# A two-block network on one Trainium2 core: the MoE's overflow branch ahead of its last pair of experts, with a hint for its jump, and the start of RWKV, the router and the layer norms rearranged

## Chip, cores, metric

The kernel runs on one core of a Trainium2 chip. The metric is device time in microseconds, the median of several executions. The profile is one execution taken by the hardware profiler. TensorE (PE) multiplies and transposes, with its weight loads shown as PEld; VectorE (DVE), ScalarE (ACT) and GpSimd (POOL) do the elementwise work; SyncE (SP) issues most transfers.

## The reference, cut to what matters

256 tokens of 1024 features pass through a first block (block-sparse attention, a convolutional feed-forward, RWKV-7 time mixing, a second feed-forward) and a second block of two layers, each a mixer (differential attention in layer 0, sparse latent attention "dsa" in layer 1), attention to a memory, and a hierarchical mixture of 16 experts. The parts that the change touches:

```python
# RWKV-7 (start)
xx = x_prev - x
xr, xw, xk, xv, xa, xg = [x + xx * mu[n] for n in range(6)]
w = -softplus(-(w0 + tanh(xw @ w1) @ w2)) - 0.5
a = sigmoid(a0 + (xa @ a1) @ a2)
g = sigmoid(xg @ g1) @ g2
...
# second block, layer i
h = layer_norm(alpha * h + mix, ...)
h = layer_norm(alpha * h + memory_cross_attention(h, ...), ...)
h = layer_norm(alpha * h + hierarchical_moe(h, ...), ...)
...
# hierarchical_moe: 4 groups of 4 experts
g_logits = t @ w_group + b_group          # best group, its softmax weight
e_logits = (t @ w_expert + b_expert)      # of that group the best two experts
combine = one_hot(expert_id) * top_w
for e in range(16):
    hid = silu(t @ w_gate[e]) * (t @ w_up[e])
    y = y + combine[:, e:e+1] * (hid @ w_down[e])
```

## The kernel before

The kernel is one straight program for the five engines, written with a tile framework: a scheduler orders each engine's instructions by program order and readiness, `tc.issue_after(ins)` puts instructions behind `ins` on its engine, and semaphores come from the data. All products before the MoE that decide the routing are made from a high and a low half in fp32r (`split`: ACT casts, DVE subtracts; three matmuls of `mm3`, L230 to L232) or in plain fp32.

**The MoE (`moe`).** Each expert takes up to 64 tokens. `route` (L1611) multiplies the router's weights with the transposed tokens into 20 rows of logits, copies them out (`lt`, L1613) and transposes them back (L1614). `choose` finds group, experts and each token's place (`pos`) on DVE in tiny instructions, and in the same pass the gate weights `C`, `Co` and the largest count `cnti`. `select` makes 0/1 matrices from `pos` (L1688), `gather` multiplies them with `hh` and `hl`, the two halves of the tokens (L1674 on ACT, L1675 on DVE), into `xg`. The loop over `q` takes two experts side by side: 64 gate and up matmuls (L1736), SiLU and product, four transposes, 32 down matmuls (L1782), the scaled results `Y` (L1789 on ACT, L1790 on DVE), and `scatter` (L1722), which adds them into four PSUM banks `acc`, a round later. `deep_add` (L403) adds the finished `acc` to the residual, and `layer_norm_both` (L407 ff.) normalises the two token halves together.

The experts' 100 MB a layer stream through a ring of 1 MB slots (`MoeQueue`): `fetch` issues on SP the next load as soon as a slot is free, `done` returns a slot after its last matmul. `once(pool, tag, parts, keep)` lends buffers of other pools to the ring; such a slot is used again only while more than `keep` loads remain.

If an expert got more than 64 tokens, `moe_dense` computes the overflow. It stands in `tc.If(over > 64)` at L1775, inside the last round's down matmuls; in these inputs it is jumped over. Every engine loads `over` from `cnti` into a register (L1747) and branches. A branch hint stands after the last round's gate and up matmuls (L1742). After the If, each engine adds to its semaphores what the skipped instructions would have added (EVENT_SEMAPHORE of L1775). Both layers use the label "dense".

**Layer norm.** `layer_norm` runs the token halves t = 0, 1 in turn: DVE adds the residual with a row sum (L372), makes the mean (L374), ACT squares with the mean as bias (L378), DVE scales (L382), two tiny DVE instructions make variance plus epsilon (L383, L384), POOL the power -1/2 (L385), DVE shifts (L391). Then `to_T` transposes (L265), ACT copies out (L277), and `route` follows. `layer_norm_both` has the same steps at L412 to L428.

**RWKV's start (`rwkv`).** After the first feed-forward come six small loads into `prow` (mixing factors and parameter rows), turned by one transpose (L628); the low-rank weights `w1`, `a1`, `g1`; `rms`; the shifted difference `xv` (L656, L657); and `mixed` (L660), one DVE instruction of 128x256 for each slab of 128 features: 8 for `xr`, 8 for `xk`, 24 for the three low-rank inputs of `lora`, whose 24 matmuls are at L671, 8 for the values. The main projections `rkp` (L236) use `xr` and `xk`.

**dsa's start.** Four loads of `b_w_in_2` by `self.load`, a `split` for each of 8 slabs, and three products a slab with the tokens.

## Time and profile before

| what | value |
|---|---|
| median of 3 runs | 1677.26 us (1676.26 to 1682.25) |
| profiled execution: its own time | 1680.34 us |
| its span, first to last instruction | 1678.5 us |
| PE busy | 1584.2 us (94%) |
| DVE busy | 856.2 us (51%) |
| ACT busy | 658.6 us (39%) |
| POOL busy | 63.3 us (4%) |
| mean granted TensorE clock | 0.971 |

Times in rows are microseconds from the start of the span unless marked ns. A line number is the kernel's. `x16` is a count of instructions merged into a row; an fp32 matmul shows as two. What stands in brackets is the engine's idle time before the row and what ended it. PEq, DVEq and so on are the engines' sequencers.

### The profile page before, as it was taken

The numbers are of one execution on the slowest core, as the hardware profiler recorded it, in microseconds if no ns is written. First come the engines' busy times: TensorE is split into PE (matmuls) and PEld (weight loads), VectorE is DVE, ScalarE is ACT, GpSimd is POOL, SyncE is SP. The second block draws the span as 40 slices with busy tenths as digits, with TensorE's granted clock in tenths as the row PEclk, the third lists the DMA queues.
The fourth block names the chain that finished last, engine by engine and source line by source line (L and its number), as shares of the span: only waits on it lengthen the run. The fifth ranks groups of instructions, "written<-read, shape, count | busy, mean of one in ns | idle before, by whom it ended". The sixth has DMA issues, their size and how long they took to land. (4 is left out here: it accounts for less than half of the span.)

```text
span 1678.5 us, 24550 instructions
## 1 busy us (share of the span) xinstructions
PE 1584.2 (94%) x9775; PEld 1160.6 (69%) x9775; DVE 856.2 (51%) x1849; ACT 658.6 (39%) x1236; POOL 63.3 (4%) x80
## 2 busy tenths in 40 slices
PE   7999999989999999999999898999968989899996
PEld 6878999958767659999888685444427768544442
DVE  5777666475665338666558645212226954421122
ACT  5776555323334236554457452111116644211111
POOL 0000000001100000000100200000000020000000
PEclk9999999989899998999999999999989999999998
DMA  9524645333223348653471855999968266599994
GB/s 345 178 76 152 226 158 169 79 92 107 85 75 108 115 138 276 204 173 126 182 270 51 336 193 209 417 416 415 405 250 307 76 239 267 212 416 415 416 416 156
DMA packets 163625, 375.27 MB, mean 224 GB/s; under 512 B 17188, under 2 KB 97836, under 8 KB 148908
## 3 DMA queue, kind: packets, MB, share of 16 engines
q1 hardware_dynamic: 159216, 363.79, 59.3%
q10 hardware_dynamic: 4284, 9.81, 1.7%
q8 instruction: 80, 1.31, 0.3%
q14 instruction: 45, 0.37, 0.1%
HBM read 372.52 MB, written 1.05 MB: 223 GB/s over the span
## 5 line engine op out<-in xcount | busy, mean ns | idle before, releaser
L203 DVE TENSOR_TENSOR wl<-w,wh 128x1024 fp32r<-128x1024 f32 (+1 forms) x221 | 265.0, 1208 | 187.1 <-ACT wh L202 186.6
L202 ACT CAST wh<-w 128x1024 fp32r<-128x1024 f32 (+1 forms) x221 | 227.0, 1038 | 211.1 <-PE mm L231 125.6
L1736 PE MATMUL mm<-mw,xg 128*64 128x512 f32 x1024 | 224.1, 593 | 2.2 <-DMA mw<-in_moe_w_up_dram 2.2
L232 PE MATMUL mm<-xh,wl 128*128 128x256 f32 x688 | 195.7, 284 | 0.0
L231 PE MATMUL mm<-xl,wh 128*128 128x256 f32 x688 | 195.4, 284 | 0.0
L230 PE MATMUL mm<-xh,wh 128*128 128x256 f32 x688 | 194.9, 283 | 0.4 <-ACT wh L202 0.4
L1736 PEld LDWEIGHTS mm<-mw,xg 128*64 128x64 f32 x1024 | 83.5, 137 | 138.7 <-issue 133.4
L230 PEld LDWEIGHTS mm<-xh,wh 128*128 128x128 f32 x688 | 131.1, 191 | 2.4 <-ACT wh L202 0.7
L230 PE MATMUL acc<-wh,xh 128*128 128x512 f32 x324 | 130.3, 408 | 1.7 <-ACT xh L268 1.0
L231 PEld LDWEIGHTS mm<-xl,wh 128*128 128x128 f32 x688 | 130.6, 190 | 1.9
L232 PEld LDWEIGHTS mm<-xh,wl 128*128 128x128 f32 x688 | 130.6, 190 | 0.0
L231 PE MATMUL acc<-wl,xh 128*128 128x512 f32 x324 | 129.3, 400 | 0.0
L232 PE MATMUL acc<-wh,xl 128*128 128x512 f32 x324 | 128.7, 399 | 0.0
L1782 PE MATMUL mm<-mw,hT 128*64 128x512 f32 x512 | 115.6, 595 | 3.1 <-issue 2.2
L1745 DVE TENSOR_TENSOR hid<-hid,mm 128x512 f32<-128x512 f32 x16 | 11.0, 686 | 185.9 <-PE mm L1736 185.9
L1782 PEld LDWEIGHTS mm<-mw,hT 128*64 128x64 f32 x512 | 40.1, 137 | 68.1 <-issue 67.0
L1790 DVE SCALAR_TENSOR_TENSOR Y<-mm,cs,Y 128x512 fp32r<-128x512 f32 x32 | 24.0, 750 | 115.8 <-ACT Y L1789 114.1
L230 PEld LDWEIGHTS acc<-wh,xh 128*128 128x128 f32 x324 | 61.6, 191 | 16.3 <-ACT mv L1290 1.5
L232 PEld LDWEIGHTS acc<-wh,xl 128*128 128x128 f32 x324 | 61.2, 189 | 14.2 <-DVE xl L271 0.3
L231 PEld LDWEIGHTS acc<-wl,xh 128*128 128x128 f32 x324 | 61.5, 190 | 13.1 <-DVE wl L203 0.5
L1789 ACT ACTIVATE Y<-mm,cs 128x512 fp32r<-128x512 f32 x32 | 22.0, 687 | 122.6 <-PE mm L1782 122.6
L232 PE MATMUL acc<-wh,fl 128*128 128x512 f32 x176 | 69.8, 396 | 0.0
(530 smaller groups left out, 2833.5 us busy)
## 6 DMA issues: line engine op xcount, KB each, us to landing
mw<-in_moe_w_down_dram SPq DMA_DIRECT2D x62, 1024.0 KB, 16.0
mw<-in_moe_w_gate_dram SPq DMA_DIRECT2D x58, 1024.0 KB, 8.2
mw<-in_moe_w_up_dram SPq DMA_DIRECT2D x56, 1024.0 KB, 16.8
w<-in_ffn_w_gate_dram SPq DMA_DIRECT2D x22, 1024.0 KB, 8.2
w<-in_ffn_w_up_dram SPq DMA_DIRECT2D x22, 1024.0 KB, 6.4
w<-in_ffn_w_down_dram SPq DMA_DIRECT2D x22, 1024.0 KB, 5.5
w<-in_attn_w_qkv_dram SPq DMA_DIRECT2D x12, 1024.0 KB, 15.5
w<-in_rwkv_w_rkv_dram SPq DMA_DIRECT2D x24, 512.0 KB, 4.0
```

The costliest lines, as they stand in the source:

```text
L202: nc.scalar.copy(r[0], raw)
L203: low = lambda: (lo_eng or nc.vector).tensor_tensor(r[1], raw, r[0], op=ALU.subtract)
L230: mm(out, lhs[0], rhs[0], start=start, stop=False)
L231: mm(out, lhs[0], rhs[1], start=False, stop=False)
L232: mm(out, lhs[1], rhs[0], start=False, stop=stop)
L1736: full = mm(ps[64 * e:64 * e + 64], xg[:, k, q % 2 * 128 + e * 64:q % 2 * 128 + e * 64 + 64], mq.slab(w[2 * (k // 4) + e], k % 4), start=k ...
L1745: tt(hid, hid, gu[1], op=ALU.mult)
L1782: mm(pd[hf][64 * e:64 * e + 64], hT[:, k, 64 * e:64 * e + 64], b, start=k == 0, stop=k == 3)
L1789: act.activation(y[0], pd[hf], AF.Copy, scale=cs)
L1790: vec.scalar_tensor_tensor(y[1], pd[hf], cs, y[0], op0=ALU.mult, op1=ALU.subtract)
```

## The change

The overflow branch now stands at the start of the last round, before its gate and up matmuls, with a label for each layer; `moe_dense` takes its buffers from the pool `gp` instead of `mo` and `xp`, and `gp`'s two slots stay in the weight ring only while more than 14 loads remain. The hint stands in round 6, for PE behind its last transpose and for DVE behind the copy of `hT`, and for no other engine. PE's load of `over` is placed ahead of round 2's matmuls. In the last round the first half's `Y`, its scatter and its `deep_add` stand among the second half's matmuls.

More than the branch is changed. The router's matmul has the tokens as stationary operand and gives the logits token by token, without `lt` and the transpose; the second part of `choose` (gates, `C`, `Co`, `cnti`) is a function `gate` that runs after the first gather; `hh` stands behind the second token half's squares on ACT, `hl` moves from DVE to POOL behind the second half's power. In the last layer norm before the MoE, the copies of the first half's transposes and its `route` wait for the second half's squares and power. All layer norms square with scale 1/32, with one tiny instruction fewer after the squares and one more before them. RWKV's parameter rows and low-rank weights are loaded ahead of the first feed-forward (`rwkv_ahead`) and turned in its fifth round; the low-rank products are split by the identity (x + xx mu) w = x w + xx (mu w): `part` multiplies `x32` with the plain weights, per token half inside `rms`, and `xv` with weights scaled once. For dsa the first two loads of `b_w_in_2` go into buffers of `xp` ahead of the layer norm, and its products run the first token half ahead of the second.

```diff
             if x32 is not None:
-                nc.scalar.copy(x32[sl], pv)
+                if defer is None:
+                    nc.scalar.copy(x32[sl], pv)
+                else:
+                    def full(sl=sl, pv=pv):
+                        with self.tc.issue_after(self.square):
+                            nc.scalar.copy(x32[sl], pv)
+                    defer.append(full)
...
-            nc.vector.tensor_scalar(st[:, 2:3], st[:, 0:1], st[:, 1:2], -1.0 / D, op0=ALU.add, op1=ALU.mult)
+            nc.vector.tensor_scalar(st[:, 3:4], st[:, 0:1], st[:, 1:2], -1.0 / (32 * D), op0=ALU.add, op1=ALU.mult)
+            nc.vector.tensor_scalar(st[:, 2:3], st[:, 3:4], 32.0, None, op0=ALU.mult)
...
-                self.square = nc.scalar.activation(mix[t][hf], x[:, t, sl], AF.Square, bias=st[:, 2:3],
+                self.square = nc.scalar.activation(mix[t][hf], x[:, t, sl], AF.Square, scale=1.0 / 32, bias=st[:, 3:4],
...
-            nc.vector.tensor_scalar(st[:, 3:4], st[:, 6:7], st[:, 7:8], 1.0 / D, op0=ALU.add, op1=ALU.mult)
-            nc.vector.tensor_scalar(st[:, 4:5], st[:, 3:4], 1e-5, None, op0=ALU.add)
+            nc.vector.tensor_scalar(st[:, 4:5], st[:, 6:7], st[:, 7:8], 1e-5, op0=ALU.add, op1=ALU.add)
             self.pow = nc.gpsimd.tensor_tensor(st[:, 5:6], st[:, 4:5], self.mhalf, op=ALU.pow).ins
...
+                if x32 is not None and t == 0:
+                    defer.append(lambda: after(0))
+                else:
+                    after(t)
...
-            vec.tensor_scalar(st[t][:, 3:4], st[t][:, 6:7], st[t][:, 7:8], 1.0 / D, op0=ALU.add, op1=ALU.mult)
-            vec.tensor_scalar(st[t][:, 4:5], st[t][:, 3:4], 1e-5, None, op0=ALU.add)
+            vec.tensor_scalar(st[t][:, 4:5], st[t][:, 6:7], st[t][:, 7:8], 1e-5, op0=ALU.add, op1=ALU.add)
             pool.tensor_tensor(st[t][:, 5:6], st[t][:, 4:5], self.mhalf, op=ALU.pow)
...
+                if j == 4 and extra:
+                    extra()
...
                 if 1 <= j <= nj:
                     down(j - 1, 0)
         self.pending = acc
+
+    def rwkv_ahead(self):
+        nc, i = self.nc, self.i
+        self.wx = ExitStack()
...
+        nc.sync.dma_start(prow[0:48], i["rwkv_mu"][0].rearrange("n (f p) -> (n f) p", p=128))
+        for n, name in enumerate(("rwkv_w0", "rwkv_a0", "rwkv_k_k", "rwkv_k_a")):
+            nc.sync.dma_start(prow[48 + 8 * n:56 + 8 * n], i[name][0].rearrange("(f p) -> f p", p=128))
+        nc.sync.dma_start(prow[80:88], i["rwkv_r_k"][0].rearrange("(f e) d -> f (e d)", e=2))
+        wa1 = x0.tile([128, 8, 128], F32, name="wa1")
...
+            nc.sync.dma_start(t, i[name][0].rearrange("(k p) r -> p k r", p=128))
+        par0 = x0.tile([128, 11, 8], F32, name="par0")
+
+        def turn():
+            p = self.ps()
+            nc.tensor.transpose(p[:, 0:88], prow, self.ident[0:88, 0:88])
...
+        wx = self.wx
+        par0, *low = self.low_rank
         par = one([128, 12, 8], "par")
-        p = self.ps()
-        pe.transpose(p[:, 0:88], prow, self.ident[0:88, 0:88])
-        vec.tensor_copy(par[:, 0:11], p[:, 0:88].rearrange("p (n f) -> p n f", f=8))
+        vec.tensor_copy(par[:, 0:11], par0)
...
-        for u in range(4):
+        for u in range(2):
             wload(u)
-        self.rms(h, i["norm_mix"][1], 1e-6, x32=x32)
-        self.acc_close()
+        mixing = []
+        for wt, parts in zip(low, (((1, 0, 64), (4, 64, 128)), ((5, 0, 128),))):
+            t = self.raws_tile()[:, 0:1024].rearrange("p (k r) -> p k r", k=8)
+            for n, a, b in parts:
+                tt(t[:, :, a:b], wt[:, :, a:b], par[:, MU + n].unsqueeze(2).broadcast_to([128, 8, b - a]), op=ALU.mult)
+            mixing.append(t)
+        for u in range(2, 4):
+            wload(u)
...
+        def part(ws, x, sl, stop):
+            for n, wt in enumerate(ws):
+                for k in range(8):
+                    mm(plr[0][:, n * 256 + sl.start:n * 256 + sl.stop], wt[:, k], x[:, k, sl],
+                       start=x is x32 and n == 0 and k == 0 and sl.start == 0, stop=stop and n == 1 and k == 7)
+
+        def shifted(t):
+            if t == 0:
+                plr.append(self.ps())
+            part(low, x32, slice(t * 128, t * 128 + 128), False)
+            c = max(1, t * 128)
+            for g in range(2):
+                ks = slice(4 * g, 4 * g + 4)
+                tt(xv[:, ks, c:t * 128 + 128], x32[:, ks, c - 1:t * 128 + 127], x32[:, ks, c:t * 128 + 128], op=ALU.subtract)
+                if t == 0:
+                    ts(xv[:, ks, 0:1], x32[:, ks, 0:1], -1.0, None, op0=ALU.mult)
+
+        self.rms(h, i["norm_mix"][1], 1e-6, x32=x32, between=shifted)
+        self.acc_close()
...
         def lora():
-            pw, pa_, pg = self.ps(), self.ps(), self.ps()
-            for k in range(8):
-                for n, wt, p, rows in ((1, w1, pw, slice(0, 64)), (4, a1, pa_, slice(64, 128)), (5, g1, pg, slice(0, 128))):
-                    m = mixed(n, k, x1.tile([128, 256], F32, name="xm", bufs=5))
-                    mm(p[rows, 0:256], wt[:, k], m, start=k == 0, stop=k == 7)
-            act.activation(tw[0:64], pw[0:64, 0:256], AF.Tanh)
-            act.copy(tw[64:128], pa_[64:128, 0:256])
-            act.activation(tg, pg[:, 0:256], AF.Tanh, scale=0.5)
+            part(mixing, xv, slice(0, 256), True)
+            act.activation(tw[0:64], plr[0][0:64, 0:256], AF.Tanh)
+            act.copy(tw[64:128], plr[0][64:128, 0:256])
+            act.activation(tg, plr[0][:, 256:512], AF.Tanh, scale=0.5)
...
-                mm(p[0:20, 0:128], wr[:, k], x32[:, k, t * 128:t * 128 + 128], start=k == 0, stop=k == 7)
-            lt = one([20, 128], "lt")
-            act.copy(lt, p[0:20, 0:128])
-            nc.tensor.transpose(p[:, 128:148], lt, self.ident[0:20, 0:20])
+                mm(p[:, 0:20], x32[:, k, t * 128:t * 128 + 128], wr[:, k], start=k == 0, stop=k == 7)
             if t:
...
+            rest.append(lambda: gate(t, p, gl, el, ge, st))
+
+        def gate(t, p, gl, el, ge, st):
+            gm, m, ngm, nt1, sg, s2 = (st[:, n:n + 1] for n in range(6))
             if t:
                 mm(p[:, 16:32], ones, M[:, 0], start=True, stop=False)
                 mm(p[:, 16:32], ones, M[:, 1], start=False, stop=True)
...
-                act.copy(hh[:, t], h[:, t])
-                tt(hl[:, t], h[:, t], hh[:, t], op=ALU.subtract)
+                with tc.issue_after(self.square):
+                    act.copy(hh[:, t], h[:, t])
+                with tc.issue_after(self.pow):
+                    nc.gpsimd.tensor_tensor(hl[:, t], h[:, t], hh[:, t], op=ALU.subtract)
...
-            mq.once(self.gp, "nrm", 2)
-            mq.once(self.gp, "g", 2)
+            mq.once(self.gp, "nrm", 2, keep=14)
+            mq.once(self.gp, "g", 2, keep=14)
...
+            for f in r["rest"]:
+                f()
...
+                if q == 7:
+                    with tc.If(over > 64, label="dense%d" % li, preferred_fallthrough_block=True):
+                        self.moe_dense(h, li, r["Co"])
...
+                            with tc.issue_after(loaded[0]) if q == 2 else ExitStack():
+                                full = mm(ps[64 * e:64 * e + 64], xg[:, k, q % 2 * 128 + e * 64:q % 2 * 128 + e * 64 + 64], mq.slab(w[2 * (k // 4) + e], k % 4),
...
-                if q == 7:
-                    tc.mark_branch_hint_location("dense", hint="LikelyTaken")
...
-                    over = nc.values_load(r["cnti"][0:1, 0:1], min_val=0, max_val=512)
+                    loads, (over,) = nc.values_load_multi_w_load_instructions(r["cnti"][0:1, 0:1], min_val=0, max_val=512)
+                    loaded = [n.ins for n in loads if n.ins.engine == full.engine]
...
-                vec.tensor_copy(hT, p.rearrange("p (f s) -> p f s", f=4))
+                copied = vec.tensor_copy(hT, p.rearrange("p (f s) -> p f s", f=4)).ins
+                if q == 6:
+                    for ins in (turned, copied):
+                        with tc.issue_after(ins):
+                            tc.mark_branch_hint_location("dense%d" % li, hint="LikelyTaken", engines=[ins.engine])
...
+                Y = []
...
+                def scaled(hf):
+                    y = [mo.tile([128, 512], F32R, name="Y%d%d" % (hf, n)) for n in range(2)]
+                    act.activation(y[0], pd[hf], AF.Copy, scale=cs)
+                    vec.scalar_tensor_tensor(y[1], pd[hf], cs, y[0], op0=ALU.mult, op1=ALU.subtract)
+                    Y.append(y)
...
-                    if q == 7 and n == 6:
-                        with tc.If(over > 64, label="dense", preferred_fallthrough_block=True):
-                            self.moe_dense(mo, h, li, r["Co"])
+                    if q == 7 and n == 4:
+                        scaled(0)
+                    if q == 7 and n == 7:
+                        scatter(7, 0, sT, Y)
+                        self.deep_add(h, acc, stats, 0)
...
+                for hf in range(len(Y), 2):
+                    scaled(hf)
...
+        if not last:
+            for n, tag in enumerate(("xh", "xl")):
+                raw = self.xp.tile([128, 2048], F32, tag=tag, name="raw")[:, 0:1248].rearrange("p (a f) -> p a f", a=2)
+                nc.sync.dma_start(raw, i["b_w_in_2"][0][n * 256:n * 256 + 256].rearrange("(a p) f -> p a f", p=128))
+                self.head.append(raw)
         self.layer_norm_both(h, acc, stats, li, 2, *(x or ()))
...
-                    t = mo.tile([128, 2, 512], F32, tag="xg", name="wo")
+                    t = self.gp.tile([128, 1024], F32, tag="nrm", name="wo").rearrange("p (k f) -> p k f", k=2)
...
-            hs = self.xp.tile([128, 4, 256], F32, tag="xl", name="hs")
+            hs = self.gp.tile([128, 1024], F32, tag="g", name="hs").rearrange("p (f n) -> p f n", f=4)
...
+        def cqkv(t, k):
+            self.mm3(acc[t], [a[:, k, t * 128:t * 128 + 128] for a in x], [a[:, 0:512] for a in ws[k]], k == 0, k == 7)
+
         for k in range(0, 8, 2):
-            raw = self.load(win[k * 128:k * 128 + 256].rearrange("(a p) f -> p a f", p=128), (2, 624))
-            for kk in range(2):
-                w = self.split(raw[:, kk])
-                kx = k + kk
-                for t in range(2):
-                    self.mm3(acc[t], [a[:, kx, t * 128:t * 128 + 128] for a in x], [a[:, 0:512] for a in w], kx == 0, kx == 7)
-                self.mm3(ptail[:, 0:256], [a[:, 496:624] for a in w], [a[:, kx] for a in x], kx == 0, kx == 7)
+            raw = self.head[k // 2] if self.head and k < 4 else \
+                self.load(win[k * 128:k * 128 + 256].rearrange("(a p) f -> p a f", p=128), (2, 624))
+            for kk in range(k, k + 2):
+                ws[kk] = self.split(raw[:, kk - k])
+                cqkv(0, kk)
+            if k:
+                for kk in range(k - 2 if k == 2 else k, k + 2):
+                    cqkv(1, kk)
+                    self.mm3(ptail[:, 0:256], [a[:, 496:624] for a in ws[kk]], [a[:, kk] for a in x], kk == 0, kk == 7)
...
+                with tc.issue_after(b.loaded) if run(0) else ExitStack():
+                    extra = b.rwkv_ahead() if run(2) else None
                 if run(1):
-                    b.ffn(h, 0)
+                    b.ffn(h, 0, extra)
```

## Rows read from the trace of the kernel before

**Rows 1.** The page's first line.

```profile
span 1678.5 us, 24550 instructions
```

**Rows 2.** The waits of PE: waiter, releaser, us in total, times, longest.

```profile
PE acc L1722 <- PEq L1775: 8.4, 2, 4.4
```

**Rows 3.** The timeline of PE at RWKV's start: start, us, instruction, idle before.

```profile
340.72 0.38 PE L628 MATMUL mm<-c_ident,prow 88*128 88x88 f32 x1 [4.31 <-DMA prow<-in_rwkv_r_k_dram]
340.90 3.62 PE L265 MATMUL mm<-c_ident,nrm 128*128 128x128 f32 x16
347.12 6.25 PE L236 MATMUL rkp<-xxh,w 128*128 128x256 f32 x16 [2.60 <-DVE xxh L660]
353.21 3.62 PE L236 MATMUL rkp<-xxl,w 128*128 128x256 f32 x16
...
368.17 0.48 PE L730 MATMUL mm<-tw,wa 64*128 64x256 f32 x1
```

**Rows 4.** The timeline of DVE in the same stretch.

```profile
339.02 1.41 DVE L301 SCALAR_TENSOR_TENSOR nrm<-h,rms,gb 128x512 f32<-128x512 f32 x2 [0.66 <-POOL rms L298]
...
346.58 3.25 DVE L660 SCALAR_TENSOR_TENSOR xxh<-xv,par,x 128x256 f32<-128x256 f32 x8
```

**Rows 5.** The timelines of DVE and PE from layer 0's last layer norm to its experts.

```profile
1020.37 0.21 DVE L383 TENSOR_SCALAR ln<-ln 128x1 f32<-128x1 f32 x1
...
1021.43 2.18 DVE L391 SCALAR_TENSOR_TENSOR h<-nrm,ln,gb 128x512 f32<-128x512 f32 x2 [0.53 <-POOL ln L385]
...
1028.34 0.23 PE L1614 MATMUL mm<-c_ident,lt 20*128 20x20 f32 x1
...
1032.80 0.42 DVE L1688 TENSOR_TENSOR sel<-iota,pos 128x256 fp32r<-128x256 f32 x1
...
1035.40 13.95 PE L1736 MATMUL mm<-mw,xg 128*64 128x512 f32 x64
```

**Rows 6.** Line L391 alone, the layer norm's shift: ns min/median/max, first and last start.

```profile
L391 DVE SCALAR_TENSOR_TENSOR h<-nrm,ln,gb x16: 744/1133/2827, 943.7 to 1441.0; 128x512 f32<-128x512 f32 x16
```

**Rows 7.** Groups by line on POOL, its 128x1024 subtraction: busy us, mean ns.

```profile
L203 POOL TENSOR_TENSOR wl<-mw,wh 128x1024 fp32r<-128x1024 f32 x6 | 15.8, 2648 | 5.8 <-ACT wh L202 5.8
```

**Rows 8.** The branch line L1775: ns min/median/max, first and last start.

```profile
L1775 DVEq COMPARE_BRANCH  x2: 72/72/72, 1246.1 to 1661.8; - x2
L1775 PEldq COMPARE_BRANCH  x2: 3739/3756/3774, 1246.1 to 1661.8; - x2
L1775 DVEq EVENT_SEMAPHORE  x2: 21/21/21, 1249.0 to 1664.6; - x2
```

**Rows 9.** The timelines of PE and DVE in layer 0's first, last rounds and behind them.

```profile
1058.66 13.93 PE L1736 MATMUL mm<-mw,xg 128*64 128x512 f32 x64
...
1058.76 1.62 DVE L1790 SCALAR_TENSOR_TENSOR Y<-mm,cs,Y 128x512 fp32r<-128x512 f32 x2 [7.13 <-ACT Y L1789]
...
1213.96 7.89 PE L1736 MATMUL mm<-mw,xg 128*64 128x512 f32 x34
...
1231.23 1.20 PE L1722 MATMUL acc<-Y,sT 128*128 128x512 f32 x4
...
1244.98 0.75 DVE L1790 SCALAR_TENSOR_TENSOR Y<-mm,cs,Y 128x512 fp32r<-128x512 f32 x1 [5.18 <-ACT Y L1789]
...
1250.09 1.19 PE L1722 MATMUL acc<-Y,sT 128*128 128x512 f32 x2 [4.36 <-PEq L1775]
...
1252.51 0.33 DVE L412 TENSOR_SCALAR ln<-ln 128x1 f32<-128x1 f32 x2
```

**Rows 10.** The timeline of DVE in layer 0's last layer norm.

```profile
1255.02 0.74 DVE L419 SCALAR_TENSOR_TENSOR nrm<-h,ln,gb 128x512 f32<-128x512 f32 x1
1255.68 0.15 DVE L423 TENSOR_SCALAR ln<-ln 128x1 f32<-128x1 f32 x1
```

**Rows 11.** Stretches: us, busy time by engine, granted clock, DMA share, GB/s.

```profile
1100.00:1125.00 25.00, 24.82 (x119) 11.25 (x118) 3.73 (x7) 2.34 (x4) 0.00 (x0) 1.00 1.02 415
1257.60:1261.00 3.40, 3.40 (x17) 3.10 (x17) 2.96 (x5) 1.73 (x3) 0.84 (x1) 0.50 0.81 294
```

61 lines of the change are left out of this document (24 added, 37 removed).

## The prediction, made before the change was run

> **What bounds the kernel now.** The page comes first: a span of 1678.5 us [rows 1] in which PE is busy nearly throughout and no other engine much more than half. So time can be won in two places: where PE stands still, and where PE does work that can go. The stretches tell which stages leave room. Inside the MoE there is none: from 1100 to 1125 us PE is busy for 24.82 of 25 us and the DMA engines move 415 GB/s at full share [rows 11]. The weight ring is refilled only when PE returns a slot, so a MoE that starts earlier ends earlier by as much, and one that is held in the middle ends later. One exception matters: 64 gate and up matmuls take 13.93 us in an early round, but layer 0's last round began them at 1213.96 and reached the scatter only at 1231.23 [rows 9]. That is 17.3 us, 3.3 of them waits for weights. Layer 1 has no such wait.
>
> Next the waits of PE: the scatter L1722 waits for PE's own sequencer at the branch, 8.4 us in two times [rows 2]. The timelines then show the other gaps that the change touches: RWKV's start [rows 3, 4], the way from the last layer norm to the first expert matmul [rows 5], and the stretch behind the last down matmul [rows 9, 10]. The reader is to look there for what ends each wait.
>
> **RWKV's start: 4.5 us won, 2 to 6.5.** PE stands 4.31 us for `prow`, and the transposes of both token halves queue behind it [rows 3]. The second half of `nrm` is ready at 339.02 + 1.41 = 340.43 [rows 4]; the first product with `xr` starts at 347.12, 6.7 us later. With `prow` turned long before, the first half's transposes and low-rank matmuls fill the old gap. Behind 340.43 there remain eight transposes (half of 3.62), a copy, half the differences and one mix of 3.25 / 8 = 0.41: products from about 345. In that time PE has the second half's low-rank matmuls. An fp32 instruction of 256 columns costs 3.62 / 16 = 0.226 us [rows 3], so one of 128 columns costs 0.113 (estimate), and 16 matmuls of two instructions 3.6 us, done at some 346.4. Then come 32 instructions for the first head pair (7.2), 16 matmuls of 256 columns on `xv` (7.2), and the quarter of the next pair that the old order had also done by then (1.8): 362.6, against 368.17, so 5.6. ACT now meets copies of the first half among squares of the second, so I take 4.5. Below: if the first half does not get ahead, only the shorter `lora` counts. It took 368.17 - 356.83 = 11.3 with the quarter in it, 9.5 without; 7.2 remain, which gives about 2. Above, 6.5, if the gap closes fully. The 24 mixes on DVE (9.8 us) vanish beside PE's work. The six small loads and the 1 MB of low-rank weights pass SP before the feed-forward's later loads, where PE does not wait for weights: nothing; without that cover, their 1 MB at 415 GB/s [rows 11], 2.5 us.
>
> **Router and `hl`: 2.5 us won over two layers, -2 to 6.4.** Per layer: L383 ran without idle time behind DVE's `hl` [rows 5]. Without it, with the squares ahead of `hh` and one tiny instruction of 0.21 less, the shift L391 starts about 1.0 earlier (estimate). The transpose back takes 0.23 at 1028.34 [rows 5], with its copy and hand-overs some 0.8. From there to the second `sel` at 1032.80 pass 4.2 us; about ten of some thirty DVE instructions there are `gate`'s: 1.4. In all 3.2. The new router matmul moves 20 columns but loads 128 by 128 tokens eight times; no row shows it, and I take its time as unchanged, within half a microsecond.
>
> Against this stands the place of `hl`. On POOL such a subtraction takes 2.648 us [rows 7]. Line L391 takes 0.744 us at best, and 2.827 where POOL's subtraction runs beside it [rows 6]: a DVE instruction with two SBUF inputs lost 2.1 us to one POOL instruction. `hl` of the first half is released by the very power that releases L391 of the second half; `hl` of the second half meets `choose`. I charge 2.0 a layer, near one such wait: 1.2 a layer remain, 2.5 together. Bounds: no wait, 6.4; two waits of 2.1 a layer, -2.0. The Trainium skill (SBUF — State Buffer, Who interferes with whom) says that a VectorE instruction with two SBUF inputs and a GpSimd instruction that reads SBUF exclude each other for the whole instruction, the later one waiting. The trace agrees, with 2.827 beside 0.744; by the rule alone, one full wait a layer, the part would give 2.2.
>
> **The branch: 6.0 us won, -1.9 to 9.8.** Won: PE's jump takes 3.74 us and DVE's code is there 1249.0 - 1246.1 = 2.9 us after its own [rows 8]; all four `deep_add` follow, and L412 starts at 1252.51 [rows 9]. Without the If, the last `Y` ends at 1244.98 + 0.75 = 1245.73, two scatters take 0.7, and of the four `deep_add` (2.4 together, from 1250.09 to 1252.51) two lie earlier, among matmuls: 1245.7 + 0.7 + 1.2 = 1247.6. That is 4.9 a layer, 9.8 together.
>
> Paid: the branch now stands between two rounds. `moe_dense` wants all four banks of the pool "mm"; two hold round 6's down products until `Y` is made. The first gate matmul behind the If overwrites a bank whose last reader in the skipped block is DVE, so it must wait for DVE's count, as L1722 waits for PEq now [rows 2]. DVE ends `Y` at 1058.76 + 1.62 = 1060.38, 1.7 us after PE started the next round [rows 9]; its branch came 0.4 after `Y` (1246.1 against 1245.73) [rows 8, 9]; with 0.2 for hand-overs PE stands 2.3 us, if the hints have both targets ready. If not, DVE's 2.9 come on top, 5.2, and PE's 3.74 run beside them. The clock: behind the old branch and the norm PE ran at half speed, granted 0.50 [rows 11]. A stop of 2.3 may cost up to as much again; I take 0.8. Layer 0: 3.1 fall into the 3.3 that its last round waits for weights anyway, since its last loads are issued in round 6; 0.7 charged for the clock's tail, 4.2 left. Layer 1 pays all: 4.9 - 3.1 = 1.8. Bounds: no stop, 9.8; no help from the hints and 2.3 for the clock, 7.5 a layer: 0.7 and -2.6.
>
> **Norms and dsa: 2.1 us won, 0 to 3.** In both `layer_norm_both` the power waits for L423, which stands behind an L419 of 0.74 [rows 10]. With one instruction less it does not: 0.9 a layer with the instruction itself. The added one, 0.2, runs beside ACT's squares. The early loads and the new order in dsa's first products: 0.3.
>
> **At nothing:** `keep=14`, because in layer 0 the ring's order leaves `gp` free by then and in layer 1 a load moves back by a few matmuls while the transfers are behind anyway (full share [rows 11]); PE's early register load; `moe_dense`'s buffers.
>
> **Sum.** 4.5 + 2.5 + 6.0 + 2.1 = 15.1 us. The profiled execution took 1680.34 us, its span and 1.8 around it, so its like would take 1665.2. The median of the runs, 1677.26, is 3.1 lower, and the forecast goes by it: **1662 us**.
>
> **Rivals.** (A) The hints do nothing. For: the old kernel has a hint too, and PE's jump still took 3.74 us in both layers [rows 8]. Against: the old hint has one label for two branches, and stood late. Stops of 5.2 + 0.8: layer 0 pays 2.7, layer 1 pays 6.0; the branch wins 1.1 instead of 6.0: 1667 us. The Trainium skill (Runtime: NRT & Kernel Launch, Instruction fetch mechanics) says that instructions are prefetched in sequence only and that a taken jump out of the loaded pages stalls for the fetch. By that rule this rival holds; the 3.74 agrees with it, and no run here shows a working hint. (B) POOL's `hl` costs two waits a layer, or comes late for the gather: -2.0 in place of 2.5, 1667 us. For: [rows 6, 7]. Against: the first `hh` may be cast only when L391 is half done. (C) No stop at the branch, because the block's waits lie inside it and DVE is through in time: 3.8 more, 1658 us. (D) Slower: the stop in the middle of the full stage drops PE's clock for long. Behind the old stop it was at half speed still at 1261.0, 11 us after 1250.09 [rows 9, 11]; half of that, 5.5, and 5.2 make 10.7 a layer, 18.1 after layer 0's 3.3. Against 9.8 and 9.1 elsewhere that is 1676.5, no change; slower by 0.5% needs a stop and clock loss from 15.3 a layer. No row shows one.
>
> **How the numbers follow.** Forecast 0.54 (its own range 1657 to 1668), A 0.20, B 0.12, C 0.10, D 0.04. Half a per cent is 8.4 us, about what can be told from no change: the runs of before spread over 6. Faster means below 1668.9: nearly all of the forecast, all of C, two thirds of A and B, 0.82 in all; no change 0.14, the rest of these; slower 0.04. The range goes from 1652, C with RWKV's upper bound, to 1672, A and B together.
>
> **What would show it.** Right: no wait for `prow` and the first `rkp` near 345; L1722 without a wait for PEq; a stop of 2 to 3 us before round 7's gate matmuls that ends with DVE's branch; L391 or `choose` stretched under POOL's `hl`. Wrong: a PE jump of 3.7 us in round 7 (A), the first expert matmul no earlier behind the norm (B), a low clock in round 7 (D), or weights that come later than before.

## The result and the profile after

The changed kernel takes 1687.62 us (median of 4, 1684.99 to 1689.22), the kernel before beside it 1676.76: ratio 1.0060, 95% interval 1.0039 to 1.0080. It is slower by 0.6%, where 1662 was forecast. The profiled execution took 1684.99, its span 1683.2.

The same points of the two timelines, in us, tell where:

| point | before | after | shift | stage |
|---|---|---|---|---|
| layer 0's last layer norm, power of the first half | 1013.59 | 1008.41 | -5.2 | RWKV: won 5.2 |
| layer 0's first expert matmul | 1035.40 | 1034.46 | -0.9 | router: lost 4.2 |
| norm behind layer 0's MoE, first power | 1255.98 | 1256.67 | +0.7 | MoE with branch: lost 1.6 |
| layer 1's first norm, power | 1357.31 | 1357.72 | +0.4 | dsa: won 0.3 |
| layer 1's last layer norm, power of the first half | 1432.05 | 1429.51 | -2.5 | attention: won 3.0 |
| layer 1's first expert matmul | 1454.80 | 1453.66 | -1.1 | router: lost 1.4 |
| last norm, first power | 1671.49 | 1675.62 | +4.1 | MoE with branch: lost 5.3 |
| end of the span | 1678.5 | 1683.2 | +4.7 | lost 0.6 |

The 3.0 us in layer 1's attention can't be credited to the change. Of its edits only those of the layer norm lie in that stretch, and kernels that all have them take from 71.7 to 74.6 us for it (74.7 before the change).

Nor is the router's part a fixed number. Eight kernels of this study have the changed router untouched, and their traces take 24.0 to 26.3 us a layer from the norm's power to the first expert matmul, where the kernel before took 21.8 and 22.8. The loss is 1.3 to 4.5 a layer; the 4.2 and 1.4 of the table are one trace.

RWKV's start is as wanted: `prow` is not waited for, the first product with `xr` starts at 346.25, the last low-rank matmuls take 7.07, and L773, L730 before, starts at 361.89 where it was 368.17 [rows 3], 6.3 earlier. The timeline of PE:

```profile
346.25 3.62 PE L239 MATMUL rkp<-xxh,w 128*128 128x256 f32 x16
...
353.16 7.07 PE L689 MATMUL mm<-xv,w 128*128 128x256 f32 x32
...
361.89 0.48 PE L773 MATMUL mm<-tw,wa 64*128 64x256 f32 x1
```

PE's waits around the MoE, largest first (us in total, times, longest). L1722's wait for PE's own sequencer [rows 2] is gone; the stop ahead of round 7's gate matmuls L1788 has taken its place and is nearly twice as long:

```profile
PE mm L1788 <- DVEq L1780: 15.7, 2, 8.2
PE mm L1654 <- ACT x L285: 5.5, 2, 2.8
PE mm L1682 <- DVE M L1677: 3.8, 2, 3.0
```

The branch's line, L1780 (ns min/median/max, first and last start), against [rows 8]:

```profile
L1780 SPq EVENT_SEMAPHORE  x16: 17/17/17, 1208.6 to 1623.0; - x16
...
L1780 SPq COMPARE_BRANCH  x2: 45/49/53, 1190.9 to 1605.7; - x2
L1780 PEldq COMPARE_BRANCH  x2: 1097/2280/3462, 1208.7 to 1627.9; - x2
...
L1780 ACTq COMPARE_BRANCH  x2: 45/45/45, 1214.2 to 1633.1; - x2
L1780 ACTq EVENT_SEMAPHORE  x2: 17/17/17, 1214.4 to 1633.6; - x2
L1780 DVEq COMPARE_BRANCH  x2: 78/84/90, 1215.1 to 1634.0; - x2
L1780 DVEq EVENT_SEMAPHORE  x2: 21/21/21, 1221.1 to 1639.6; - x2
```

DVE's branch comes at 1215.1, 0.3 behind its last `Y` and 1.9 behind PE's last down matmul, about as foreseen. But its first instruction in the code jumped to stands at 1221.1, 6.0 us later, and in layer 1 at 1639.6 after 1634.0, 5.6 later; before, it was 2.9. PE jumps early, while its down matmuls are still queued, and ACT has 0.2 and 0.5. So the stop is DVE's jump. The windows (busy time of PE first, then granted clock, DMA share and GB/s at the end) show what lay beside it, and what it left behind: full DMA engines, and half clock until about 1225. Before the change the jump, from 1246.1 on, lay beside idle engines; that window comes first.

```profile
1245.00:1250.00 5.00, 0.73 (x2) 0.29 (x2) 0.73 (x1) 0.00 (x0) 0.00 (x0) 1.00 0.02 7
```
```profile
1206.00:1210.00 4.00, 3.88 (x18) 1.64 (x20) 0.01 (x1) 0.00 (x0) 0.00 (x0) 1.00 0.24 94
...
1215.00:1218.00 3.00, 0.00 (x0) 0.00 (x0) 0.00 (x0) 0.00 (x0) 0.00 (x0) 0.55 1.02 431
1218.00:1221.30 3.30, 0.00 (x0) 0.00 (x0) 0.00 (x0) 0.00 (x0) 0.00 (x0) 0.50 0.99 412
1221.30:1225.00 3.70, 3.59 (x10) 1.26 (x12) 0.00 (x0) 0.00 (x0) 0.00 (x0) 0.50 1.02 421
```

The 64 gate and up matmuls then take 15.97 us in layer 0 and 16.65 in layer 1, for 13.93 [rows 9]. Behind the last round the move pays what it should: from the last `Y` to L424, 1251.06 to 1253.62, are 2.6 us, where L412 came 7.5 behind it [rows 9].

The router, on DVE, POOL and PE in layer 0:

```profile
1017.65 1.94 DVE L1668 SCALAR_TENSOR_TENSOR e<-lg,st,first 128x4 f32<-128x4 f32 x1
...
1019.82 2.08 DVE L1670 TENSOR_SCALAR e<-e,st 128x4 f32<-128x4 f32 x1
...
1016.25 5.62 POOL L1721 TENSOR_TENSOR hl<-h,hh 128x1024 fp32r<-128x1024 f32 x2 [1.16 <-issue]
...
1014.74 1.96 PE L1654 MATMUL mm<-wr,x 128*128 128x20 f32 x16 [2.76 <-ACT x L285]
...
1025.65 2.06 PE L1745 MATMUL acc<-sel,hh 128*128 128x256 f32 x8
1027.51 1.91 PE L1745 MATMUL acc<-sel,hl 128*128 128x256 f32 x8
...
1020.00:1023.00 3.00, 0.10 (x1) 0.00 (x0) 2.82 (x8) 0.39 (x2) 1.87 (x1) 0.50 0.59 235
1026.00:1029.00 3.00, 3.00 (x16) 3.00 (x15) 2.14 (x20) 0.70 (x3) 0.00 (x0) 0.50 0.65 210
```

Two instructions of `choose` on 128x4 take 1.94 and 2.08 us beside POOL's `hl` (0.22 and 0.23 without it, below). In layer 1 POOL's first instruction meets the norm's shift, two in 4.33 us where layer 0's second half has 2.21, and its second meets `choose` (L1677, 1.59). That is some 3.5 us a layer on DVE.

```profile
1015.12 2.21 DVE L400 SCALAR_TENSOR_TENSOR h<-nrm,ln,gb 128x512 f32<-128x512 f32 x2 [0.66 <-POOL ln L394]
...
1436.31 4.33 DVE L400 SCALAR_TENSOR_TENSOR h<-nrm,ln,gb 128x512 f32<-128x512 f32 x2 [0.73 <-POOL ln L394]
...
1442.57 1.59 DVE L1677 TENSOR_TENSOR M<-mr,el 128x16 f32<-128x16 f32 x1
```

And PE, idle 2.76 us for the first half's token copies, which now stand behind the second half's squares, runs the rest of router and gather in layer 0 at a granted 0.50; of its two clock levels that is 1.2 GHz. Its 32 gather matmuls take 2.06 + 1.91 + 2.06 + 1.88 = 7.9 us there, and 1.22 + 0.98 + 0.36 + 1.21 + 1.11 = 4.9 before. In layer 1 they take 6.3 and took 6.4: before, the second half ran at half clock, now the first. So the gather's loss is layer 0's alone in this pair of traces, and its clock moves from trace to trace: with the same changed router the second half's 8 matmuls with `hh` take 1.2 us in 8 of 16 layers and 2.05 in the other 8. Before, layers 0 and 1, then the changed layer 1:

```profile
1029.25 1.22 PE L1699 MATMUL acc<-sel,hh 128*128 128x256 f32 x8 [0.67 <-DVE sel L1688]
...
1451.20 1.96 PE L1699 MATMUL acc<-sel,hh 128*128 128x256 f32 x8 [0.70 <-DVE cnti L1656]
```
```profile
1451.54 1.21 PE L1745 MATMUL acc<-sel,hh 128*128 128x256 f32 x8
```

### The profile page after: what moved, and what is told of

It is laid out like the page before. It is cut to its first block, busy times and chain, and to the rows that moved or that the text cites. A ratio compares the mean times of both kernels' runs of the same rounds, so it can differ in the third digit from the quotient of the medians.

```text
span 1683.2 us, 24625 instructions
## 1 busy us (share of the span) xinstructions
PE 1589.3 (94%) x9819; PEld 1170.3 (70%) x9819; DVE 853.7 (51%) x1827; ACT 657.7 (39%) x1232; POOL 75.1 (4%) x84
## 5 line engine op out<-in xcount | busy, mean ns | idle before, releaser
L1788 PE MATMUL mm<-mw,xg 128*64 128x512 f32 x1024 | 227.6, 603 | 15.7 <-DVEq L1780 15.7
L1788 PEld LDWEIGHTS mm<-mw,xg 128*64 128x64 f32 x1024 | 82.1, 139 | 157.5 <-issue 157.3
```

What stands on the lines that cost most here:

```text
L1788: full = mm(ps[64 * e:64 * e + 64], xg[:, k, q % 2 * 128 + e * 64:q % 2 * 128 + e * 64 + 64], mq.slab(w[2 * (k // 4) + e], k % 4), start=k ...
```

## The experiments

Each kernel is the changed one with the edit named; ratios are to the kernel before, run beside it (its medians were 1675.9 to 1679.6, so ratios compare better than times).

| run | edit | us | ratio, 95% |
|---|---|---|---|
| e1_old_place | branch at its old place | 1677.96 | 0.9995, 0.9980 to 1.0010 |
| e3_loop | overflow block as a loop | 1673.77 | 0.9975, 0.9962 to 0.9987 |
| e4_no_branch | no branch | 1673.81 | 0.9979, 0.9966 to 0.9992 |
| e7_drain | e3, block's loads on POOL's queue | 1673.67 | 0.9968, 0.9953 to 0.9983 |
| e10_quiet | loads of round 7 held | 1693.23 | one run |
| e16_no_loads | no loads for round 7 | 1678.62 | one run |
| e11_nohint | no hints | 1688.78 | one run |
| e2_hl_dve | `hl` on DVE | 1684.15 | 1.0036, 1.0022 to 1.0050 |
| e5_copies | copies early | 1685.80 | 1.0039, 1.0025 to 1.0054 |
| e6_copies_dve | copies early and `hl` on DVE | 1682.26 | 1.0010, 0.9999 to 1.0020 |
| e14_router_alone | router's old matmul | 1681.46 | 1.0020, 1.0010 to 1.0030 |
| e8_all | e7 and e6 | 1667.40 | 0.9921, 0.9904 to 0.9937 |
| e9_old_router | e8, router's old matmul | 1667.35 | 0.9947, 0.9930 to 0.9964 |
| e12_loop_old_place | e8, branch at its old place | 1665.37 | 0.9934, 0.9910 to 0.9957 |
| e15_both_undone | old place, the router's three edits undone | 1670.49 | 0.9956, 0.9939 to 0.9973 |
| e13_best | e12, router's old matmul | 1661.03 | 0.9889, 0.9869 to 0.9909 |

### The branch

**Back to the old place.**

```diff
-                if q == 7:
-                    with tc.If(over > 64, label="dense%d" % li, preferred_fallthrough_block=True):
...
+                    if q == 7 and n == 6:
+                        with tc.If(over > 64, label="dense%d" % li, preferred_fallthrough_block=True):
```

> The changed kernel with the overflow branch alone put back to its old place in the last round, behind the first six groups of down matmuls, and its two hints one round later, as far ahead of it as before; all else is as changed. Theory, the stop: the moved branch stops PE 8.2 and 7.5 us ahead of round 7's gate matmuls and costs 2.0 and 2.7 us of half clock behind it, less some 3.3 us that layer 0 waits for weights anyway, while it wins 5.1 to 5.5 us a layer behind the last down matmul. So putting it back gains 17.1 and loses 10.6: about 1681 us, 6.5 below the changed kernel. Rival, the move itself is good and all the loss is elsewhere (the hl subtraction on POOL): the old place costs its 4.9 a layer again, about 1697 us.

Measured 1677.96: undoing the move wins 0.65% or 10.9 us, more than the 6.5 expected. The old place is cheaper than it was: PE's jump takes 0.52 us in layer 0, and PE's wait for its sequencer fell from 8.4 us in two times [rows 2] to 3.0 in one. Whether the early register load, the hint or the earlier `Y` does that was not separated. DVE's jump, with the same block and hint but the DMA engines nearly idle (7 and 10 GB/s in the two stretches), takes 3.0 and 3.1 us (the branch's line, then the windows):

```profile
L1837 DVEq COMPARE_BRANCH  x2: 78/84/90, 1239.3 to 1659.1; - x2
L1837 DVEq EVENT_SEMAPHORE  x2: 21/21/21, 1242.2 to 1662.2; - x2
```
```profile
1239.00:1242.30 3.30, 0.70 (x2) 0.30 (x2) 0.00 (x0) 0.00 (x0) 0.00 (x0) 0.71 0.03 7
1659.00:1662.20 3.20, 0.23 (x2) 0.19 (x2) 0.07 (x1) 0.00 (x0) 0.00 (x0) 0.69 0.04 10
```

**The block as a loop.** The built program's block has 192 instructions on DVE and 1332 on PE; as a loop under 40 and some 125. No token overflows in this data, so neither form of it ever runs.

```diff
-        for e in range(16):
+        with self.tc.For_i(0, 16, 1) as e:
...
-                    nc.sync.dma_start(t, w[e, c * 256:c * 256 + 256].rearrange("(k p) f -> p k f", p=128))
+                    nc.sync.dma_start(t, w[bass.ds(e, 1), c * 256:c * 256 + 256].rearrange("o (k p) f -> p (o k) f", p=128))
```

> The changed kernel with the sixteen experts of the overflow block written as a loop: the skipped block shrinks from 192 to under 40 instructions on VectorE and from 1332 to some 125 on TensorE; place, hints and all else stay. Theory, the jump fetches: VectorE's branch target lies outside the code that is already there, and the fetch takes 6.0 and 5.6 us beside a full DMA; with a target a few instructions on there is no fetch, VectorE's part of the stop falls to under 0.7 us, PE's stop to about 2 us a layer (VectorE's Y and the branch), and little clock is lost: 13 us won, about 1674.5 us. Rival 1, the stop is the wait of all the engines for the semaphores of the skipped block or a late register load, whatever its length: unchanged, 1687.5 us.

Measured 1673.77, as expected. DVE's jump takes 0.7 and 0.2 us, PE's 0.4, and the stop is 2.8 and 2.1 us, the 2.3 of the prediction:

```profile
L1780 PEldq COMPARE_BRANCH  x2: 371/384/397, 1208.7 to 1624.6; - x2
...
L1780 DVEq COMPARE_BRANCH  x2: 78/86/94, 1215.1 to 1630.7; - x2
L1780 DVEq EVENT_SEMAPHORE  x2: 21/21/21, 1215.8 to 1630.9; - x2
```
```profile
PE mm L1788 <- DVEq L1780: 4.9, 2, 2.8
```

**No branch at all** (the `with`, its body and the two hints are dropped).

> The changed kernel without the overflow branch (the overflow work is left out; no token overflows in this data). The bound of what a branch can cost: by the theory of the stop 8.2 + 2.0 - 3.3 and 7.5 + 2.7 us go, 17.1 in all, and about 1670.5 us remain; what it lies below the loop's kernel is the price of a branch that jumps within loaded code, about 2 us a layer. By the rival (the loss is at the router) it stays within 3 us of 1687.

Measured 1673.81, no better than the loop. PE, earlier by the stop, now waits for round 7's weights instead, in both layers:

```profile
PE mm L1785 <- DMA mw<-in_moe_w_up_dram: 4.4, 4, 1.4
```

The medians say that the loop's stop of some 2 us a layer costs nothing that the intervals (some 2 us each) resolve. They do not say that the weight stream is the bound. In e12 and e13 below, with the loop at the old place, PE enters round 7 with neither a stop nor a wait for weights. There SP issues round 7's first up load 17 us ahead of the round (1193.7 for 1211.2 in e12), here 3.8 (1202.9 for 1206.7). What holds these loads back in e4 is not shown.

**What makes the jump long.** Two runs were to let DVE jump beside idle DMA engines at the new place. The first held the last loads until the gate matmuls were done.

> The changed kernel with the last loads of round 7's weights held until its first gate matmuls are done, so that the DMA engines are idle while VectorE jumps. Theory, a full DMA makes the fetch late: VectorE's branch to its semaphore instruction takes 2.9 us as in the kernel before, not the 6.0 and 5.6 of the changed one, and PE's stop falls from 8.2 to about 5. The whole gets slower, since round 7 waits for its weights: only the jump is looked at. Rival, the fetch is longer because of its place or its hint: 5.5 to 6 us again.

It missed: two gate loads and some of the held ones still ran, the engines moved 429 GB/s from 1217 to 1220, and the jump took 6.1 us, so it separates nothing. The second leaves the loads out:

```diff
-        for p in range(8):
+        for p in range(7):
...
+                if q == 7:
+                    mq.used -= 12
```

> The changed kernel without the loads of round 7's weights (left out: its last two experts run with the weights of the two before, so the output is not the reference's). The DMA engines are then idle when VectorE jumps at the new place, with the same block and hint. If the full DMA makes the fetch slow: VectorE's branch to its semaphore instruction takes 2.9 to 3.1 us as at the old place, and PE's stop falls from 8.2 and 7.5 to about 5. If the place or the hint makes it slow: 5.5 to 6 us again.

Measured: 3.1 and 2.8 us for the jump, stops of 5.2 and 4.6, at 3 and 5 GB/s. Place, block and hint are the changed kernel's, so the full DMA is what doubles the jump. All traces with the unrolled block agree: eight jumps beside idle engines take 2.8 to 3.1 us, at either place, and fourteen beside full ones 5.4 to 6.6. The branch's line, a window of the first jump, and PE's waits:

```profile
L1782 DVEq COMPARE_BRANCH  x2: 78/84/90, 1211.0 to 1632.7; - x2
L1782 DVEq EVENT_SEMAPHORE  x2: 21/21/21, 1214.1 to 1635.5; - x2
```
```profile
1210.00:1213.00 3.00, 0.00 (x0) 0.00 (x0) 0.65 (x1) 0.00 (x0) 0.00 (x0) 0.85 0.01 3
```
```profile
PE mm L1790 <- DVEq L1782: 9.8, 2, 5.2
```

**Without hints** (both `mark_branch_hint_location` calls dropped).

> The changed kernel without its two hints. Theory: VectorE's hint does nothing (no instruction transfer of its queue follows it), so VectorE's jump stays at 5.5 to 6 us and the stop at 7.5 to 8.2; TensorE's hint brings its code early, so without it TensorE's branch takes 4 us or more in both layers where it took 1.1 and 3.5, hidden behind the queued down matmuls; time unchanged within 1.5 us of the changed kernel. Rival, VectorE's hint does harm (a wrong fetch first): its jump falls to about 3 us and the stop to 5.

Measured: DVE's jump 5.4 and 6.6 us, as with its hint; PE's branch 3.7 and 6.2 us, with its hint 1.1 and 3.5. DVE's hint does nothing: six other kernels with it have 5.4 to 6.5. PE's brings 2.6 and 2.8 us that lie hidden behind the down matmuls; this rests on one run without hints, and its two branches are longer than those of the six unrolled kernels with a hint beside full DMA engines (0.7 to 1.2 in layer 0, 3.3 to 3.7 in layer 1). The time lies within the four runs of the changed kernel.

```profile
L1780 PEldq COMPARE_BRANCH  x2: 3674/4950/6225, 1207.2 to 1631.5; - x2
...
L1780 DVEq COMPARE_BRANCH  x2: 72/72/72, 1213.6 to 1637.6; - x2
L1780 DVEq EVENT_SEMAPHORE  x2: 21/21/21, 1219.0 to 1644.2; - x2
```

**SP at the branch.** SP's branch in the changed kernel comes at 1190.9 and the semaphore instructions behind it at 1208.6; the DMA engines then fall to 94 GB/s (the windows above). In the trace's records each of SP's eight semaphore instructions behind the If waits for one semaphore of its loads before it adds to it, and the last data in flight lands at 1208.1.

```diff
-                    nc.sync.dma_start(t, w[bass.ds(e, 1), ...
+                    nc.gpsimd.dma_start(t, w[bass.ds(e, 1), ...
```

> The loop's kernel with the loads of the overflow block on POOL's queue in place of SP's. Theory, the drain: where SP jumps over a block that holds loads it first waits until all its earlier loads have landed (branch at 1190.9, its semaphore instructions at 1208.6 us), so the DMA engines fall to 94 GB/s between 1206 and 1210 in a stage that lives on 415; layer 0's round 7 then takes 17.3 us where 64 matmuls take 13.95. With nothing of SP's in the block there is no drain: the loads run on through 1200 to 1215, round 7 has its weights, and 3 us in layer 0 and 0 to 1.7 in layer 1 are won: about 1670 us. Rival, the dip comes from ring slots that PE has not returned yet: dip and time stay, 1673.8.

The dip is gone, at 414 GB/s in the same stretch; the time is the loop's within the intervals, and 3 us were expected. In the trace layer 0's MoE, from the first expert matmul to the norm's first power, takes 216.3 us where e3 has 218.8, and layer 1's 215.7 and 215.6. The drain is real; what it costs is at most those 2.4 us in layer 0, which the times don't resolve.

```profile
1206.00:1210.00 4.00, 4.00 (x22) 1.75 (x20) 0.00 (x0) 0.00 (x0) 0.00 (x0) 1.00 1.01 414
```

### The router

**`hl` on DVE**, both halves behind `M` of the first.

```diff
-                with tc.issue_after(self.pow):
-                    nc.gpsimd.tensor_tensor(hl[:, t], h[:, t], hh[:, t], op=ALU.subtract)
+                with tc.issue_after(r["m0"]):
+                    tt(hl[:, t], h[:, t], hh[:, t], op=ALU.subtract)
```

> The changed kernel with hl computed on VectorE again, both halves behind the first half's M of the router; the branch stays where the change put it. Theory, two locks: in layer 0 two tiny VectorE instructions of choose took 1.94 and 2.08 us beside POOL's 5.62 us of hl, and the first expert matmul came 4.2 us later behind the norm than before; in layer 1 1.4 us. Without POOL's hl none of the tiny instructions is above 0.3 us and the way from the last norm to the first expert matmul shrinks by 4 us in layer 0 and 2 to 3 in layer 1: about 1681 us (1679 to 1683). Rival, POOL's hl lies beside other work and the loss there has another cause (the order of the router's matmuls): under 1.5 us, 1686 to 1688.

Half a miss: the lock is gone (L1668 and L1670 at 0.22 and 0.23), but only 0.24% or 4 us are won of 6.6, and the intervals of the two kernels overlap. In the trace the way from the norm to the first expert matmul is 1.4 shorter in layer 0 and 0.8 longer in layer 1. PE still runs the gather at half clock, and it waits for `sel`, which now stands behind the second `hl`:

```profile
1025.06 2.08 PE L1747 MATMUL acc<-sel,hh 128*128 128x256 f32 x8 [1.80 <-DVE sel L1736]
```

**Copies early**: `full` is not put behind the squares.

```diff
-                    def full(sl=sl, pv=pv):
-                        with self.tc.issue_after(self.square):
-                            nc.scalar.copy(x32[sl], pv)
-                    defer.append(full)
+                nc.scalar.copy(x32[sl], pv)
```

> The changed kernel with one line group undone: the router's fp32 copies of the first token half on ACT are no longer put behind the second half's squares. Theory, the clock: in the changed kernel PE stands 2.8 us a layer for these copies while ACT is idle for 4.6 us ahead of the squares; after that its granted clock is 0.50 through router and gather, so that the 32 gather matmuls of a layer take 7.8 us where they took 4.3. With the copies early the wait falls under 1 us and the gather is back near 4.5 us at least in one layer; POOL's lock on choose stays. 2 to 3 us a layer, about 1683 us. Rival, the router's new matmuls (20 columns for a load of 128 by 128) drop the clock by themselves: the gather stays at 0.50 and the gain is under 1.5 us in all.

> Both changes at the router: copies early, and hl on VectorE behind M. Theory, the lock and the slow clock each hide the other, which is why hl on VectorE alone won only 3 us: together they win 4 to 6 us a layer, about 1677 us, and the way from the second half's power to the first expert matmul falls from 19.9 and 18.0 us to below 15. Rival (the clock falls by the router's matmuls themselves): 1682 or more, gather at 0.50.

What the rival foresaw of the clock came both times: the gather's first half stays at half clock in both layers of both kernels, and its second half in all but layer 1 of e5. With copies early alone 0.21% are won, with overlapping intervals; with both, 0.50%, clear of them, and the way from the second half's power to the first expert matmul is 17.3 us, not below 15. That the router's form is the cause does not follow (see e14). The wait for the copies is gone, but in e5 PE waits for the second half's norm instead, up to 4.8 us:

```profile
1018.51 2.15 PE L268 MATMUL mm<-c_ident,h 128*128 128x128 f32 x8 [4.79 <-DVE h L394]
...
1030.78 2.06 PE L1739 MATMUL acc<-sel,hh 128*128 128x256 f32 x8
```

**The router's old matmul**, first in the kernel with all other cures, then alone in the changed one.

```diff
-                mm(p[:, 0:20], x32[:, k, t * 128:t * 128 + 128], wr[:, k], start=k == 0, stop=k == 7)
+                mm(p[0:20, 0:128], wr[:, k], x32[:, k, t * 128:t * 128 + 128], start=k == 0, stop=k == 7)
+            lt = one([20, 128], "lt")
+            nc.scalar.copy(lt, p[0:20, 0:128])
+            nc.tensor.transpose(p[:, 128:148], lt, self.ident[0:20, 0:20])
```

> The last kernel (loop, block's loads on POOL's queue, copies early, hl on VectorE) with the router's matmul turned back: the 20 router columns are loaded and 128 tokens move, and the logits are copied and transposed back as before the change. Theory, the clock hangs on the router's form: with 20 moving columns PE's granted clock is 0.50 from the second half's transposes through the gather (gather of 32 matmuls 7.8 us in both kernels with the copies early or late); with 128 moving columns the clock is back at 1.00 by the gather as in the kernel before, 32 gather matmuls take under 5 us, and of 3.3 us a layer some 0.8 to 1 go to the transpose back: 2 us a layer, about 1663 us. Rival, the clock falls because PE waits 2.7 us for the second half's norm, whatever the router's form: gather at 0.50 and the time 1 to 2 us longer, 1668 to 1669.

> The changed kernel with the router's matmul alone turned back to 128 moving tokens; copies late, hl on POOL and the branch as changed. If the router's form alone drops the clock: gather back at a granted 1.00 in both layers, about 3 us a layer less, 1 us a layer for the transpose back, 1683 us. If the wait of 2.8 us for the late copies or POOL's lock is enough to drop it: gather at 0.50 still, 1687 to 1689.

With the cures layer 0's gather is back at full clock (1.22 and 1.21 for 8 matmuls) and the first expert matmul comes 3.2 us earlier; layer 1's is still slow in its first half, and the time, 1667.35, is that of e8 and not the 1663 expected. Alone the old form leaves layer 0's gather at half clock (timelines of PE, the kernel with all cures first):

```profile
1023.25 1.22 PE L1744 MATMUL acc<-sel,hh 128*128 128x256 f32 x8 [0.60 <-DVE sel L1733]
...
1026.29 1.21 PE L1744 MATMUL acc<-sel,hh 128*128 128x256 f32 x8
```
```profile
1020.25 2.08 PE L1748 MATMUL acc<-sel,hh 128*128 128x256 f32 x8
...
1025.41 2.05 PE L1748 MATMUL acc<-sel,hh 128*128 128x256 f32 x8
```

Alone it still wins 0.4% against the changed kernel. But its trace has the 4 us already ahead of layer 0's last norm, and the router's way itself is 0.8 shorter in the two layers, so how much of the 0.4% is the router's stays open.

What holds for the clock is weak. In every layer of the 14 changed kernels that lack one or more of the three edits, the gather's first half runs at half clock. With all three (e9, e13, e15) it runs at full clock throughout in three layers of six, at half clock in its first half in two, and at half clock throughout in one. The kernel before had half clock in one half of four. The old form with only one of the other two edits was not run.

### Together

> The changed kernel with both losing parts undone and nothing new: the unrolled overflow block at its old place, hl on VectorE, copies early, the router's old matmul; RWKV's start, the norms and dsa stay as changed. If branch and router are all of the loss, what remains is RWKV's 5.9 us and 1 to 3 us of the norms: 1668 to 1670 us. If a third part loses too, 1673 or more.

Measured 1670.49, ratio 0.9956. Branch and router are the whole loss as far as the times resolve: what is left of the change wins 0.44%, 7.4 us, where RWKV and the norms had won 5.2 and 0.4 a layer in the changed kernel's trace. From 1.0060 to 0.9995 the branch costs 10.9 us, and from 0.9995 to 0.9956 the router 6.5, each to some 4 us.

> All of it on the changed kernel: loop, the block's loads on POOL's queue, copies early, hl on VectorE. If the three causes (VectorE's jump, SP's drain, router with slow clock and lock) are separate they add: 1687.5 - 13.7 - 3.5 - 10 = 1660 us. If the weight stream of the MoE (415 GB/s from its first to its last round) takes over as the bound, the early start is given back as waits for weights in round 7, and it stays at 1665 to 1668.

> The same four edits as in the last kernel but with the branch at its old place behind the first six groups of down matmuls. With a block of 40 to 125 instructions a jump costs under 0.7 us wherever it stands, so the old place loses little at the end, and the stop of 2.8 us with 1.5 us of slower clock ahead of round 7 is gone: 3 us a layer less than at the new place, 1661 to 1663 us. Rival, the stop at the new place is hidden by weights that come late anyway: within 1.5 us of 1667.4.

> All that the runs so far speak for, in one kernel: RWKV's and the norms' part of the change; the overflow block as a loop with its loads on POOL's queue, at the old place; copies early, hl on VectorE, and the router's matmul in its old form. The kernel with the loop at the old place took 1665.4 us with a gather at half clock; the old router form started layer 0's first expert matmul 3.2 us earlier in the profile of the run before. If that start is carried to the end: 1662 us, 1 per cent below the kernel before. If round 7 gives it back as waits for weights: 1665.

The cures add up only in part: e8 came to 1667.4, where 1660 stood for a full sum and 1665 to 1668 for a weight stream that takes some of it back. The time fits the second, the trace only in part: the MoE is 12.0 us shorter than in the changed kernel, where 17.2 were to go, with one wait for weights of 2.1 in round 7, and the router's way is 4.3 shorter, where 10 were to go.

The place still counts once the block is short. The traces with loop and POOL's queue have 1.9 to 2.6 us a layer less in the MoE at the old place: 213.9 and 213.1 in e12 for 216.5 and 215.8 in e8, 214.0 and 213.1 in e13 for 215.9 and 215.8 in e9. What goes is the stop, the slow clock behind it and layer 1's wait for weights. Round 7 in layer 0 of e9 (new place) and e13 (old):

```profile
1209.98 14.96 PE L1787 MATMUL mm<-mw,xg 128*64 128x512 f32 x64 [2.80 <-DVEq L1779]
```
```profile
1207.30 14.24 PE L1784 MATMUL mm<-mw,xg 128*64 128x512 f32 x64
```

The times do not settle how much: e13 and e9 differ by 0.58%, clear of their intervals, e12 and e8 by nothing beyond them (0.9934 and 0.9921). The last kernel, with everything, takes 1661.03 beside 1678.33: 1.1% faster than the kernel before, 1.7% faster than the changed one by the ratios.

## Why the prediction was wrong, step by step

**The branch's price failed.** "PE stands 2.3 us, if the hints have both targets ready. If not, DVE's 2.9 come on top, 5.2." Place, waiter and cause were right (a gate matmul waits for DVE's count), and 2.3 is what remains when the jump is short (2.8 and 2.1 in e3). The price of the jump was taken from [rows 8], where it lay beside idle DMA engines. At the new place the weights fill them: 6.0 and 5.6, and 2.8 to 3.1 when they are emptied (e16) or at the old place (e1). The forecast also counted on the hints to make DVE's target ready; DVE's hint did nothing (e11). The clock was charged with 0.8 and cost 2.0 and 2.7. Stop and clock together came to 10.2 a layer, where 3.1 was taken and 7.5 was to be the upper bound.

The Trainium skill (Runtime: NRT & Kernel Launch, Instruction fetch mechanics) says that a taken jump stalls when its target is not among the code pages already loaded. The runs agree: 5.6 to 6.0 us over 192 instructions, 0.2 to 0.7 over fewer than 40.

**The branch's gain and layer 0's cover held.** The way behind the last down matmul was to shrink by 4.9 a layer; from the last `Y` to L412 or L424 it fell from 7.5 to 2.6, 4.9. Layer 0's 3.3 us of weight waits were absorbed: round 7 has no wait for weights after. With 6.0 forecast, -6.9 came (1.6 and 5.3 lost, the norms' 0.4 a layer included): 4.9 - 10.2 + 3.3 and 4.9 - 10.2 give -2.0 and -5.3.

**Router and `hl` failed**: 2.5 forecast, -5.6 measured. The lock was foreseen, on the norm's L391 and on `choose`, but charged with one wait a layer, 2.0. It came twice in each: on `choose` in layer 0 (1.94 and 2.08), on the shift, L400 now, and on `choose` in layer 1, 3.5 a layer in all. With it alone the part would be near nothing (3.2 - 3.5 a layer). The larger slip is the sentence that the new router matmul's "time [is] unchanged" together with "the squares ahead of `hh`": it overlooked that the token copies go behind the squares too, so that PE stands 2.8 us a layer, and that PE's clock has a part in this stretch at all, 3.0 us of gather in layer 0. The lower bound of -2.0 did not hold either. How the remaining loss splits between wait, lock and clock was not separated.

The Trainium skill (SBUF — State Buffer, Who interferes with whom) lets a VectorE and a GpSimd instruction that share a port exclude each other for the whole length. The trace agrees: two 128x4 instructions take 1.94 and 2.08 us beside POOL's two, 5.62 together, and 0.22 and 0.23 without POOL.

**RWKV and norms.** RWKV: 4.5 forecast; 6.3 at L773, near the 5.6 worked out before the charge for ACT, and 5.2 left at the last norm of layer 0, both within its 2 to 6.5. Norms: 0.9 a layer forecast, 0.4 found in layer 0 (L412 to the first power 3.5 before, L424 to it 3.1 after). For dsa the 0.3 of the table is the forecast, but the stretch takes 100.8 to 101.8 us in the kernels of this study, so it is not shown.

**The start of the argument** held where a pair of traces tests it. "A MoE that starts earlier ends earlier by as much": layer 0's starts 3.2 us earlier in e9 than in e8 and ends 3.8 earlier, and in e13 it starts 3.6 earlier than in e12 and ends 3.6 earlier. In e4 a wait of 4.4 us for weights takes the place of the stop, for a reason that stays open.

**The rivals.** Half of A came true (DVE's hint does nothing, PE's works), and B did, with a larger price. D's price of stop and clock, 10.7 a layer, is nearly what was measured, 10.2, but by luck: its parts were 5.2 for the stop and 5.5 for the clock, measured 7.5 to 8.2 and 2.0 to 2.7. It stood at 0.04 because it was to reach 15.3 with the rest of the sum as forecast. D with the router's measured -5.6 in place of 2.5 gives 1676.5 + 8.1 = 1684.6, 7.3 above the median of the kernel before. The traces differ by 4.7, or 7.7 without layer 1's attention, the medians by 10.9. The two mechanisms were weighed one at a time, and their sum was not. Of the signs of being wrong three came: PE's branch of 3.5 us (in layer 1), the first expert matmul later behind the norm, and a low clock in round 7.
